# Spatial gating on Trainium2: the u projection and the token mixing with channels on the partitions

## The chip, the cores and the metric

The kernel runs on one core of one Trainium2 chip. The metric is the device time of one execution in microseconds (us). Engines: PE (TensorE; PEld are its weight loads), DVE (VectorE), ACT (ScalarE), POOL (GpSimd), SP (SyncE, which issues the DMAs). A matmul holds one operand of up to 128 x 128 still in the array, loaded ahead of it, and moves the columns of the other past it; the result goes to PSUM, here in banks of 128 x 512 f32.

## The reference

A trunk of two layers on 256 tokens of 1024 channels. Each layer is SwiGLU, a mixer, SwiGLU, with a layer norm behind each. The mixer of the first layer is the spatial gating at issue:

```
z = gelu(x @ w_in + b_in)            # 256 x 4096
u, v = split(z, 2, axis=-1)          # 256 x 2048 each
v = layer_norm(v, ln_g, ln_b)
v = v.reshape(1, 2, 128, 16, 128)    # 2 chunks of 128 tokens, 16 groups of 128 channels
w = where(causal, w_sp, 0)           # 16 x 128 x 128, token by token
mixed = einsum('gts,bcsgd->bctgd', w, v) + b_sp.T[None, None, :, :, None]
out = (u * mixed.reshape(1, 256, 2048)) @ w_out
```

The mixer of the second layer is an RWKV-7 time mixing, which the change leaves alone.

## The kernel before, in words

**Products.** Weights are f32. A `Stream` brings them in units of 128 x 1024 in the order of their use: SP loads a unit (L90) into one of 4 staging tiles `raw`, ACT rounds it to fp32r (`wh`, L113) and DVE takes the rest (`wl`, L114). A ring of 4 places, with 6 more while there is room, holds the split units; a staging tile is free again, and the next load may start, when its unit is split. Activations are split likewise (`split`, L206 to L208). `mm3` (L199 to L203) makes a product of three fp32r matmuls: rounded by rounded, and twice rounded by rest.

**Order.** The stage is written as a list of ops; `run` issues them in order, and ahead of each splits the units that have a place. PE and SP execute in this order. The order on ACT and DVE is set by the scheduler, so a wait on either holds what is queued behind it.

**The spatial gating (`sgu`, L440 to L620).** Tokens are on the partitions, in two blocks `m` of 128. `to_cm` (L218) transposes x for use as the still operand: `xh`, `xl`, channels by tokens. `proj_both` (L304) makes 512 columns of a projection for both blocks in four quarters, each with two of the four units of a part: block 0, block 1, block 0, block 1. The still operand is x (128 channels by 128 tokens), and 512 weight columns move past it. There are two PSUM banks `mm` for this, so each part needs the banks of the part before.

1. Four parts of v (key `sv`): `vdone` (L482) adds the bias on DVE, applies GELU on ACT, and gathers statistics; `vln` normalises v in place, four times two passes over 1024 columns (L252, L253).
2. Four parts of u (key `su`, p = 0 to 3): `udone` (L513) adds the bias on DVE (L521) and applies GELU on ACT (L522).
3. `M(p)` (L525): per token block, four products of a group's transposed causal weights `wspT` with v, in f32 (L532; each shows as two matmuls in the trace), into a bank `tp`; then four fused steps on DVE, (mixed + b_sp) * u, with b_sp one number per token, that is per partition (L538).
4. `T(p)` (L542): the gated u is transposed for the output projection, 8 transposes (L547), and split on ACT and DVE (L207, L208) into `pT`.
5. `O(p, i, m)` (L553): six matmuls with `pT` as the still operand and 512 columns of w_out moving, accumulating into four banks `acc`.

M and T of a part stand between quarters of later parts, or between O's.

Of the kernel before, what the change touches and what calls it, by code (L numbers as in the profile page):

```python
# [22 lines left out]
P = 128  # L23
D = 1024
# [30 lines left out]
class Stream:  # L55
    """Weight units in the order of their use: each is loaded ahead of time and split
    exactly into a rounded part and the rest, which one-pass products carry."""
# [12 lines left out]
    def free(self, now, v):  # L70
        """The next place of the ring for unit v, if the work issued up to op `now` is done with it."""
        shut = min((i for i in self.shut if i > now), default=1 << 30)
        n = N_W + (N_WX if self.ext and self.last[v] < shut else 0)
        for d in range(n):
            t = (self.turn + d) % n
            u = self.ring[t]
            if u is None or self.last[u] <= now:
                return t
        return None

    def load(self, now, upto=None):
        """Load what the staging places allow after the work issued up to op `now`."""
        while len(self.loaded) < (upto or len(self.units)):
            v = len(self.loaded)
            o = v - N_RAW
            if o >= 0 and (len(self.done) <= o or o in self.native and self.last[o] > now):
                break
            t = self.raw.tile([P, 1024], F32, tag="raw", name=f"raw{v}")
            for view, src in self.units[v]:
                self.nc.sync.dma_start(view(t), src)  # L90
            self.loaded.append(t)

    def advance(self, now, ahead, upto=None):
# [24 lines left out]
        assert upto is None or upto < len(self.done), "no place for a weight unit"  # L118
# [4 lines left out]

class Builder:
# [14 lines left out]
    def extra(self, kind):  # L139
        """The room next to the lasting pools: more weight units, or more 4 KB tiles."""  # L140
# [11 lines left out]
    def flush(self):  # L152
        """The last normalisation of the stage before, behind the first work of this one."""
# [64 lines left out]
    def to_cm(self, src):  # L218
        """[tokens, channels] -> rounded part and rest, [channel, block of channels, token]."""
# [52 lines left out]
    def proj(self, ps, m, xs, key, us):  # L272
        """ps[128 tokens, 512] += x[m] @ units us of key (two blocks of 128 rows each)."""
        for u in us:
            h, l = self.w((key, u))
            for k in range(2):
# [5 lines left out]
                else:  # L282
                    i = self.mm3(ps, xs[0][:, c], xs[1][:, c], h[:, s], l[:, s], kk == 0, kk == 7)
# [20 lines left out]
    def proj_both(self, key, xs, done, between=None):  # L304
        """Both token blocks, two units at a time; between[i]: ops before the i-th quarter."""
# [134 lines left out]
    def sgu(self, S):  # L440
# [9 lines left out]
        st = {"xs": [None, None], "p": {}, "pT": {}, "u": {}, "n": [0, 0], "bc": {}}  # L450

        def cm(m):
            def f():
                st["xs"][m] = self.to_cm(S["x"][m])
# [7 lines left out]
        def start2():  # L462
# [6 lines left out]
            bs = self.small("bsp", [16, P])  # L469
            nc.sync.dma_start(bs, a["sgu_b_sp"][0])  # L470
            st["wsp"], st["bsn"] = wsp, bs
# [6 lines left out]
        def start4():  # L478
            st["bu"] = [self.bcast(bin_[h * D:(h + 1) * D], "bu") for h in range(2)]
# [27 lines left out]
        def bspT():  # L507
            ps = self.tpb()
            nc.tensor.transpose(ps[:, :16], st["bsn"], self.ident[:16, :16])
            st["bsp"] = self.small("bspT", [P, 16])  # L510
            nc.vector.tensor_copy(st["bsp"], ps[:, :16])

        def udone(p):  # L513
            def f(m, ps):
                if (p, 0) not in st["u"]:
                    t = self.s4("u")
                    for mm in range(2):
                        st["u"][p, mm] = t[:, mm * 512:mm * 512 + 512]
                u = st["u"][p, m]
                h, s = p // 2, slice((p % 2) * 512, (p % 2) * 512 + 512)  # L520
                nc.vector.tensor_tensor(u, ps, st["bu"][h][:, s], op=ALU.add)  # L521
                nc.scalar.activation(u, u, AF.Gelu)  # L522
            return f

        def M(p):  # L525
            def f():
                for m in range(2):
                    ps = self.tpb()
                    for i in range(4):
                        g = 4 * p + i  # L530
                        o = slice((g % 8) * P, (g % 8) * P + P)
                        nc.tensor.matmul(ps[:, i * P:i * P + P], lhsT=st["wT"][g // 8][:, o],  # L532
                                         rhs=st["v"][m][g // 8][:, o], start=True, stop=True)
                    for i in range(4):
                        g = 4 * p + i
                        s = slice(i * P, i * P + P)
                        u = st["u"][p, m][:, s]
                        nc.vector.scalar_tensor_tensor(u, ps[:, s], st["bsp"][:, g:g + 1], u,  # L538
                                                       op0=ALU.add, op1=ALU.mult)
            return f  # L540

        def T(p):  # L542
            def f():
                for m in range(2):
                    ps = self.tpb()
                    for i in range(4):
                        nc.tensor.transpose(ps[:, i * P:i * P + P], st["u"][p, m][:, i * P:i * P + P], self.ident)  # L547
                    t = self.s4("pT", F32R)
                    self.split(t[:, 0:512], t[:, 512:1024], ps)
                    st["pT"][p, m] = t  # L550
            return f

        def O(p, i, m):  # L553
            def f():
                t = st["pT"][p, m]
                n0 = st["n"][m]
                wh, wl = self.w(("so", 4 * p + i))
                for n in range(2):
                    s = slice(n * 512, n * 512 + 512)
                    self.mm3(st["acc"][m][n], t[:, i * P:i * P + P], t[:, 512 + i * P:512 + i * P + P],  # L560
# [25 lines left out]
        self.proj_both(("sv", 3), xs, vdone(3), {1: [bspT]})  # L586
# [5 lines left out]
        def group(p, m_, t_):  # L592
            for i in range(4):
                O(p, i, 0)
                O(p, i, 1)
                if i == 0:
                    self.op(m_)
                if i == 2:
                    self.op(t_)
# [23 lines left out]
    def rwkv(self, S):  # L623
        """The loads and the preparation that may come before the stage, and the stage."""
# [106 lines left out]
        def lora1(m):  # L731
            """The first products of both small nets, with a row of ones below for the second's bias."""
# [35 lines left out]
        def decay_x(m):  # L768
            """What stood before each token: the row above, or 1 at the start of a chunk."""
# [8 lines left out]
        def decay_w(m):  # L778
            """A chunk's last row is the decay of the whole chunk."""
# [131 lines left out]
        def cm_kb(m, i, q):  # L911
            """Chunk 0 has its keys before its b's, chunk 1 behind."""
# [146 lines left out]
        class Chunk:  # L1059
            """One chunk of 64 tokens; v's in the half of the partitions that is the chunk's, u's in the other."""  # L1060
# [308 lines left out]
```

## Time and profile before

| what | value |
|---|---|
| median of 3 runs | 1148.21 us (1146.11 to 1149.02) |
| profiled execution, span from first to last instruction | 1146.8 us |
| PE busy | 1103.2 us, 96% |
| weight loads busy (PEld) | 878.3 us, 77% |
| DVE busy | 698.1 us, 61% |
| ACT busy | 481.2 us, 42% |
| DMA, mean | 189 GB/s |
| granted TensorE clock, mean over the span | 0.987 |

The profile is one execution of its own. Its span is 1146.8 us, and the time of that execution from outside is not among the numbers shown; the runs' median lies 1.4 us above the span, their lowest 0.7 below it. A busy time is the union of an engine's records. Records of matmuls, and of weight loads, overlap: the mean of one says how long it was under way, and the distance between starts says what it cost. The granted clock is 1.00 at 2.4 GHz and 0.50 at 1.2 GHz.

### The profile page before, as it was taken

The numbers are of one execution on the slowest core, as the hardware profiler recorded it, in microseconds if no ns is written. First come the engines' busy times: TensorE is split into PE (matmuls) and PEld (weight loads), VectorE is DVE, ScalarE is ACT, GpSimd is POOL, SyncE is SP. The second block draws the span as 40 slices with busy tenths as digits, with TensorE's granted clock in tenths as the row PEclk, the third lists the DMA queues.
The fourth block names the chain that finished last, engine by engine and source line by source line (L and its number), as shares of the span: only waits on it lengthen the run. The fifth ranks groups of instructions, "written<-read, shape, count | busy, mean of one in ns | idle before, by whom it ended". The sixth has DMA issues, their size and how long they took to land.

```text
span 1146.8 us, 15330 instructions
## 1 busy us (share of the span) xinstructions
PE 1103.2 (96%) x5854; PEld 878.3 (77%) x5854; DVE 698.1 (61%) x964; ACT 481.2 (42%) x632; POOL 42.3 (4%) x44
## 2 busy tenths in 40 slices
PE   7999999999999999999999999999989889999997
PEld 5788888778888888888788888775555768888885
DVE  5654556769658555457655453878655788555544
ACT  5544444455335444444444452462123145444430
POOL 0000000100000000000000000112100110000000
PEclk9999999999999999999999999999998999999999
DMA  8776565776644766655567563437876135766631
GB/s 277 244 236 187 182 196 168 233 254 201 215 147 151 243 204 199 187 184 154 189 218 224 184 199 125 165 93 251 269 203 222 60 123 190 245 201 196 184 111 37
DMA packets 153788, 216.51 MB, mean 189 GB/s; under 512 B 21197, under 2 KB 114829, under 8 KB 153714
## 3 DMA queue, kind: packets, MB, share of 16 engines
q1 hardware_dynamic: 152250, 210.80, 57.5%
q0 software_dynamic: 1024, 3.15, 1.0%
q10 hardware_dynamic: 440, 1.57, 0.5%
q8 instruction: 46, 0.75, 0.3%
q14 instruction: 28, 0.23, 0.1%
HBM read 209.46 MB, written 3.42 MB: 186 GB/s over the span
## 4 chain that ended last, share of the span: by engine, by line
PE 77%; DVE 8%; DMA 7%; issue 3%; ACT 2%; SPq 1%; POOL 1%; ACTq 0%; DVEq 0%; POOLq 0%
PE mm L201 14%; PE mm L203 14%; PE mm L202 14%; PE acc L201 8%; PE acc L203 8%; PE acc L202 8%; PE mm L281 3%; DMA raw<-ffn_w_in 3%; DVE wl L114 2%; PE tp L376 2%; ACT wh L113 1%; DMA raw<-sgu_w_in 1%; POOL rs L239 1%; SPq L90 1%; PE tp L215 1%
## 5 line engine op out<-in xcount | busy, mean ns | idle before, releaser
L114 DVE TENSOR_TENSOR wl<-raw,wh 128x1024 fp32r<-128x1024 f32 x328 | 396.2, 1221 | 272.7 <-ACT wh L113 264.7
L113 ACT CAST wh<-raw 128x1024 fp32r<-128x1024 f32 x328 | 340.4, 1051 | 347.7 <-PE acc L203 144.1
L201 PE MATMUL mm<-wh,xh 128*128 128x512 f32 x832 | 327.6, 394 | 8.3 <-DVE h L366 3.8
L202 PE MATMUL mm<-wl,xh 128*128 128x512 f32 x832 | 325.1, 391 | 1.2 <-DVE wl L114 1.2
L203 PE MATMUL mm<-wh,xl 128*128 128x512 f32 x832 | 325.1, 391 | 0.2 <-DVE xl L208 0.2
L201 PEld LDWEIGHTS mm<-wh,xh 128*128 128x128 f32 x832 | 156.6, 188 | 44.9 <-DVE h L366 5.5
L202 PEld LDWEIGHTS mm<-wl,xh 128*128 128x128 f32 x832 | 156.6, 188 | 34.8 <-DVE wl L114 3.2
L203 PEld LDWEIGHTS mm<-wh,xl 128*128 128x128 f32 x832 | 156.5, 188 | 34.4 <-DVE xl L208 1.9
L201 PE MATMUL acc<-wh,hT 128*128 128x512 f32 x352 | 140.9, 400 | 0.0
L203 PE MATMUL acc<-wh,hT 128*128 128x512 f32 x352 | 137.6, 391 | 0.0
L202 PE MATMUL acc<-wl,hT 128*128 128x512 f32 x352 | 137.2, 390 | 0.0
L365 ACT ACTIVATE h<-mm 128x256 f32<-128x256 f32 x88 | 33.8, 384 | 104.1 <-PE mm L203 104.1
L203 PEld LDWEIGHTS acc<-wh,hT 128*128 128x128 f32 x352 | 66.1, 188 | 14.3
L202 PEld LDWEIGHTS acc<-wl,hT 128*128 128x128 f32 x352 | 66.3, 188 | 12.8
L201 PEld LDWEIGHTS acc<-wh,hT 128*128 128x128 f32 x352 | 66.1, 188 | 12.5
L366 DVE TENSOR_TENSOR h<-h,mm 128x256 f32<-128x256 f32 x88 | 36.7, 417 | 58.8 <-ACT h L365 58.8
L281 PE MATMUL mm<-raw,mix 128*128 128x512 f32 x128 | 60.6, 619 | 0.7 <-DMA raw<-rwkv_w_rkv 0.7
L239 POOL TENSOR_TENSOR rs<-ve,mhalf 128x1 f32<-128x1 f32 x14 | 14.1, 1010 | 928.0 <-DVE ve L247 928.0
L281 PEld LDWEIGHTS mm<-raw,mix 128*128 128x128 f32 x128 | 24.0, 196 | 27.2 <-issue 25.1
L208 DVE TENSOR_TENSOR hT<-tp,hT 128x512 fp32r<-128x512 f32 x44 | 30.1, 684 | 7.6 <-ACT hT L207 7.6
L207 ACT CAST hT<-tp 128x512 fp32r<-128x512 f32 x44 | 25.8, 587 | 9.0 <-PE tp L376 8.9
L261 DVE SCALAR_TENSOR_TENSOR y<-acc,x 128x512 f32<-128x512 f32 x24 | 15.9, 685 | 18.7 <-PE acc L203 18.7
(189 smaller groups left out, 878.4 us busy)
## 6 DMA issues: line engine op xcount, KB each, us to landing
raw<-ffn_w_in SPq DMA_DIRECT2D x352, 256.0 KB, 3.9
raw<-ffn_w_out SPq DMA_DIRECT2D x88, 512.0 KB, 3.9
raw<-rwkv_w_rkv SPq DMA_DIRECT2D x40, 512.0 KB, 4.0
raw<-sgu_w_in SPq DMA_DIRECT2D x32, 512.0 KB, 4.9
raw<-sgu_w_out SPq DMA_DIRECT2D x16, 512.0 KB, 3.5
raw<-rwkv_w_o SPq DMA_DIRECT2D x8, 512.0 KB, 3.5
lng<-ln_g SPq DMA_DIRECT2D x6, 512.0 KB
lnb<-ln_b SPq DMA_DIRECT2D x6, 512.0 KB
```

What stands on the lines that cost most here:

```text
L113: nc.scalar.copy(h, raw)
L114: nc.vector.tensor_tensor(l, raw, h.bitcast(F32), op=ALU.subtract)
L201: i = mm(out, lhsT=lh, rhs=rh, start=start, stop=False)
L202: mm(out, lhsT=lh, rhs=rl, start=False, stop=False)
L203: mm(out, lhsT=ll, rhs=rh, start=False, stop=stop)
L207: self.nc.scalar.copy(h, src)
L208: self.nc.vector.tensor_tensor(l, src, h.bitcast(F32), op=ALU.subtract)
L239: self.nc.gpsimd.tensor_tensor(rs, v, self.mhalf[:, :w], op=ALU.pow)
L281: i = self.nc.tensor.matmul(ps, lhsT=xs[:, c], rhs=h[:, s], start=kk == 0, stop=kk == 7)
L365: nc.scalar.activation(hb[:, o + 256:o + 512], ps[:, 0:256], AF.Silu)
L366: nc.vector.tensor_tensor(hb[:, o:o + 256], hb[:, o + 256:o + 512], ps[:, 256:512], op=ALU.mult)
L376: nc.tensor.transpose(ps[:, o:o + P], st["h"][c][:, hh:hh + P], self.ident)
```

## The change

The u projection changes sides. The weights are the still operand (128 channels of input by 128 columns of u, one group), and the 256 tokens of both blocks move past them, so u comes out with channels on the partitions. For this x is kept as a `Pair`: four tiles that hold both token blocks beside each other; the v projections read one block of them as before. `U(p)` takes the place of `proj_both` and `udone`: two ops of 48 matmuls, one for units 0 and 1, one for 2 and 3, each over the four groups of the part; two groups share a bank. In the second op GELU follows each group on ACT, from PSUM, with b_in as its bias per partition. `M(p, j)` mixes two groups of both token blocks with v as the still operand, so that the result has channels on the partitions too; DVE adds b_sp (now broadcast over the partitions, as b_in was), multiplies by u, and the product is split straight into `pT`. `T` is gone. The loads of b_in and b_sp change places.

```diff
+class Pair:
+    def __init__(self, b):
+        self.b = b
+        self.h = [b.s4("xh", F32R) for q in range(2)]
+        self.l = [b.s4("xl", F32R) for q in range(2)]
+
+    def fill(self, src, m):
+        def evac(q, ps):
+            at = lambda t: t.rearrange("p (k m t) -> p k m t", k=4, m=2)[:, :, m, :]
+            self.b.split(at(self.h[q]), at(self.l[q]), ps.rearrange("p (k t) -> p k t", k=4))
+        self.b.transpose8(src, evac)
...
+    def both(self, k):
+        o = (k % 4) * 256
+        return self.h[k // 4][:, o:o + 256], self.l[k // 4][:, o:o + 256]
...
-            st["bu"] = [self.bcast(bin_[h * D:(h + 1) * D], "bu") for h in range(2)]
+            bsp = a["sgu_b_sp"][0].rearrange("g t -> (g t)")
+            st["bsp"] = [self.bcast(bsp[h * D:(h + 1) * D], "bsb") for h in range(2)]
...
+        def U(p, between=None):
+            ps = []
+            def go(us):
+                def f():
+                    if us[0] == 0:
+                        ps[:] = [self.mmb(), self.mmb()]
+                        st["u"][p] = self.s4("u")
+                    ws = [self.w((("su", p), u)) for u in us]
+                    for g in range(4):
+                        out = ps[g // 2][:, (g % 2) * 256:(g % 2) * 256 + 256]
+                        for u, (h, l) in zip(us, ws):
+                            for k in range(2):
+                                xh, xl = st["X"].both(2 * u + k)
+                                c = slice(k * 512 + g * P, k * 512 + g * P + P)
...
+                                mm(out, lhsT=h[:, c], rhs=xh, start=first, stop=False, skip_group_check=True)
+                                mm(out, lhsT=l[:, c], rhs=xh, start=False, stop=False, skip_group_check=True)
+                                mm(out, lhsT=h[:, c], rhs=xl, start=False, stop=last, skip_group_check=True)
+                        if us[-1] == 3:
+                            o = g * 256
+                            nc.scalar.activation(st["u"][p][:, o:o + 256], out, AF.Gelu,
+                                                 bias=st["bu"][:, 4 * p + g:4 * p + g + 1])
+                return f
...
-        def T(p):
...
-                        nc.tensor.transpose(ps[:, i * P:i * P + P], st["u"][p, m][:, i * P:i * P + P], self.ident)
...
+        def M(p, j):
+            def f():
+                ps = self.tpb()
+                for i in range(2):
+                    g = 4 * p + 2 * j + i
+                    c = slice((g % 8) * P, (g % 8) * P + P)
+                    for m in range(2):
+                        o = (i * 2 + m) * P
+                        nc.tensor.matmul(ps[:, o:o + P], lhsT=st["v"][m][g // 8][:, c],
+                                         rhs=st["wT"][g // 8][:, c], start=True, stop=True)
...
+                nc.vector.tensor_tensor(e4(x), e4(ps), b.unsqueeze(2).broadcast_to([P, 2, 2, P]), op=ALU.add)
+                u = st["u"][p][:, j * 512:j * 512 + 512]
+                nc.vector.tensor_tensor(u, u, x, op=ALU.mult)
+                t = self.s4("pT", F32R)
+                self.split(t[:, 0:512], t[:, 512:1024], u)
+                st["pT"][p, j] = t
...
-        self.proj_both(("su", 0), xs, udone(0), {1: [vln(0, 0)], 2: [vln(0, 1)], 3: [vln(1, 0)]})
-        self.proj_both(("su", 1), xs, udone(1), {1: [vln(1, 1)]})
-        self.proj_both(("su", 2), xs, udone(2), {1: [M(0)], 3: [T(0)]})
+        U(0, {1: [vln(0, 0), vln(0, 1)]})
+        U(1, {0: [vln(1, 0)], 1: [vln(1, 1)]})
+        U(2, {0: [M(0, 0)], 1: [M(0, 1)]})
...
-        group(0, M(1), T(1))
-        self.proj_both(("su", 3), xs, udone(3), {1: [M(2)], 3: [T(2)]})
+        group(0, M(1, 0), M(1, 1))
+        U(3, {0: [M(2, 0)], 1: [M(2, 1)]})
         self.op(gb)
         self.ahead = 99
-        group(1, M(3), T(3))
+        group(1, M(3, 0), M(3, 1))
```

**PE, from the end of the second u part into the third.** Before, the mixing block of part 0 (L532; `vz` is v, `wspT` the causal weights) stands after the first quarter of the third part, and a block of transposes (L547) after its third:

```order
L203 MATMUL mm<-wh_2129,xl_1604 128x512
L532 MATMUL tp<-vz_1593,wspT_1696 128x128 [waits PE_49]
L532 MATMUL tp<-vz_1593,wspT_1696 128x128 x3
L532 MATMUL tp<-vz_1595,wspT_1696 128x128 x4
L201 MATMUL mm<-wh_2123,xh_1723 128x512 [waits DVE_49]
...
L203 MATMUL mm<-wh_2169,xl_1604 128x512
L547 MATMUL tp<-ident,u_2098 128x128 [waits DVE_49,Activation_49]
L547 MATMUL tp<-ident,u_2098 128x128 x3
```

Now half a block (L589) stands ahead of the third part, whose matmuls are 256 columns wide (L565 to L567):

```order
L567 MATMUL mm<-xl_1606,wh_2014 128x256
L589 MATMUL tp<-wspT_1698,vz_1593 128x128 [waits DVE_49,PE_49]
L589 MATMUL tp<-wspT_1698,vz_1595 128x128 [waits DVE_49]
L589 MATMUL tp<-wspT_1698,vz_1593 128x128
L589 MATMUL tp<-wspT_1698,vz_1595 128x128
L565 MATMUL mm<-xh_1603,wh_2171 128x256
L566 MATMUL mm<-xh_1603,wl_2172 128x256
L567 MATMUL mm<-xl_1605,wh_2171 128x256
```

The block moved ahead of the part's first matmul and was halved, and the transposes have no successor.

**ACT, from the second u part on.** Before (L113 rounds a weight, L522 is GELU of u, L207 the split of the transposed product; numbers tell tiles apart):

```order
L113 CAST wh_2260<-raw_2167 128x1024 [waits DMAHW7_49,PE_49,Activation_49]
L113 CAST wh_2266<-raw_2173 128x1024 [waits DMAHW0_49,PE_49,Activation_49]
L522 ACTIVATE u_2187<-u_2187 128x512 [waits DVE_49]
L113 CAST wh_2317<-raw_2208 128x1024 [waits DMAHW1_49,PE_49,Activation_49]
L113 CAST wh_2353<-raw_2214 128x1024 [waits DMAHW2_49,PE_49,Activation_49]
```

Now (L570 is GELU, from the bank `mm` and with the bias):

```order
L113 CAST wh_2317<-raw_2181 128x1024 [waits DMAHW6_49,Activation_49]
L570 ACTIVATE u_2185<-mm,bspT 128x256 [waits PE_49,Pool_49]
L113 CAST wh_2385<-raw_2240 128x1024 [waits DMAHW7_49,Activation_49]
L570 ACTIVATE u_2185<-mm,bspT 128x256 [waits PE_49]
L113 CAST wh_2391<-raw_2246 128x1024 [waits DMAHW0_49,Activation_49]
L570 ACTIVATE u_2185<-mm,bspT 128x256 [waits PE_49]
L113 CAST wh_2449<-raw_2315 128x1024 [waits DMAHW1_49,PE_49,Activation_49]
```

GELU was two passes that waited for DVE and freed no bank; it is now four that wait for PE and free PE's banks, each behind the copy of a weight that waits for a DMA.

## Rows read from the trace of the kernel before

**Rows 1.** Page's head: span, and each engine's busy us (share) xinstructions

```profile
span 1146.8 us, 15330 instructions
...
PE 1103.2 (96%) x5854; PEld 878.3 (77%) x5854; DVE 698.1 (61%) x964; ACT 481.2 (42%) x632; POOL 42.3 (4%) x44
```

**Rows 2.** Stretch: length; PE, PEld, DVE, ACT, POOL busy; clock, DMA, GB/s

```profile
251.00:327.00 76.00, 75.95 (x383) 63.81 (x382) 61.43 (x90) 36.17 (x44) 2.91 (x2) 1.00 0.60 198
```

**Rows 3.** Chain of waits from 190 to 360 us: start us, us, what

```profile
276.55 1.78 PE tp L532 x16
...
283.80 0.87 PE tp L547 x8
...
324.56 0.87 PE tp L547 x8
```

**Rows 4.** Timeline of PE, first two u parts: start us, us, engine, line

```profile
253.85 0.39 PE L203 MATMUL mm<-wh,xl 128*128 128x512 f32 x1
254.18 0.50 PE L201 MATMUL mm<-wh,xh 128*128 128x512 f32 x1
254.52 0.39 PE L202 MATMUL mm<-wl,xh 128*128 128x512 f32 x1
...
262.25 0.39 PE L203 MATMUL mm<-wh,xl 128*128 128x512 f32 x1
262.69 0.47 PE L201 MATMUL mm<-wh,xh 128*128 128x512 f32 x1
263.00 0.40 PE L202 MATMUL mm<-wl,xh 128*128 128x512 f32 x1
```

**Rows 5.** Timeline of PE at a mixing block and at a transpose block

```profile
276.39 1.95 PE L532 MATMUL tp<-vz,wspT 128*128 128x128 f32 x16
278.09 0.48 PE L201 MATMUL mm<-wh,xh 128*128 128x512 f32 x1
278.41 0.40 PE L202 MATMUL mm<-wl,xh 128*128 128x512 f32 x1
...
283.64 1.03 PE L547 MATMUL tp<-ident,u 128*128 128x128 f32 x8
...
284.74 0.40 PE L202 MATMUL mm<-wl,xh 128*128 128x512 f32 x1
```

**Rows 6.** Weight loads by line: xcount | busy us, mean ns | idle before, releaser

```profile
L202 PEld LDWEIGHTS mm<-wl,xh 128*128 128x128 f32 x832 | 156.6, 188 | 34.8 <-DVE wl L114 3.2
...
L532 PEld LDWEIGHTS tp<-vz,wspT 128*128 128x128 f32 x64 | 7.8, 191 | 0.3
```

**Rows 7.** DVE and ACT groups, the same view

```profile
L113 ACT CAST wh<-raw 128x1024 fp32r<-128x1024 f32 x328 | 340.4, 1051 | 347.7 <-PE acc L203 144.1 <-PE mm L203 126.3 <-DMA raw<-ffn_w_in 30.0
...
L365 ACT ACTIVATE h<-mm 128x256 f32<-128x256 f32 x88 | 33.8, 384 | 104.1 <-PE mm L203 104.1
...
L538 DVE SCALAR_TENSOR_TENSOR u<-tp,bspT,u 128x128 f32<-128x128 f32 x32 | 8.8, 343 | 4.7 <-PE tp L532 4.7
...
L521 DVE TENSOR_TENSOR u<-mm,bu 128x512 f32<-128x512 f32 x8 | 5.5, 685 | 1.2 <-PE mm L203 1.2
...
L522 ACT ACTIVATE u<-u 128x512 f32<-128x512 f32 x8 | 5.0, 632 | 4.9 <-DVE u L521 4.8
```

**Rows 8.** Timelines of DVE and ACT, 253 to 270 us

```profile
253.44 0.68 DVE L486 TENSOR_TENSOR vz<-mm,bv 128x512 f32<-128x512 f32 x1
...
259.47 2.47 DVE L253 SCALAR_TENSOR_TENSOR vz<-vz,rs,slb 128x1024 f32<-128x1024 f32 x2
...
261.86 0.68 DVE L521 TENSOR_TENSOR u<-mm,bu 128x512 f32<-128x512 f32 x1
...
268.06 1.22 DVE L114 TENSOR_TENSOR wl<-raw,wh 128x1024 fp32r<-128x1024 f32 x1
...
269.44 1.05 ACT L113 CAST wh<-raw 128x1024 fp32r<-128x1024 f32 x1 [5.40 <-DMA raw<-sgu_w_out]
```

**Rows 9.** DMA issues, 200 to 327 us: xcount, KB each, median us to landing

```profile
raw<-sgu_w_out SPq DMA_DIRECT2D x16, 512.0 KB, 3.5
```

More of the change, by code (lines that the diff above doesn't have):

```diff
@@ L121, in get, with block, at @@
         return self.done[i]
+class Pair:
[8 more added lines that the diff above has]
+        self.b.transpose8(src, evac)
+    def block(self, m):
+        def at(k):
+            o = (k % 4) * 256 + m * P
+            return self.h[k // 4][:, o:o + P], self.l[k // 4][:, o:o + P]
+        return at
+    def both(self, k):
+        o = (k % 4) * 256
+        return self.h[k // 4][:, o:o + 256], self.l[k // 4][:, o:o + 256]
 class Builder:
@@ L282, in proj @@
                 else:
-                    i = self.mm3(ps, xs[0][:, c], xs[1][:, c], h[:, s], l[:, s], kk == 0, kk == 7)
+                    xh, xl = xs(kk) if callable(xs) else (xs[0][:, c], xs[1][:, c])
+                    i = self.mm3(ps, xh, xl, h[:, s], l[:, s], kk == 0, kk == 7)
                 self.first.setdefault(key, i)
@@ L449, in sgu @@
             self.def_rows(("so", g), wout[g * P:(g + 1) * P, :])
-        st = {"xs": [None, None], "p": {}, "pT": {}, "u": {}, "n": [0, 0], "bc": {}}
+        st = {"xs": [None, None], "pT": {}, "u": {}, "n": [0, 0]}
         def cm(m):
             def f():
-                st["xs"][m] = self.to_cm(S["x"][m])
+                if m == 0:
+                    st["X"] = Pair(self)
+                st["X"].fill(S["x"][m], m)
+                st["xs"][m] = st["X"].block(m)
             return f
@@ L468, in start2 @@
                                         base=0, channel_multiplier=1)
-            bs = self.small("bsp", [16, P])
-            nc.sync.dma_start(bs, a["sgu_b_sp"][0])
-            st["wsp"], st["bsn"] = wsp, bs
+            bu = self.small("bsp", [16, P])
+            nc.sync.dma_start(bu, bin_[0:DSGU].rearrange("(g p) -> g p", p=P))
+            st["wsp"], st["bun"] = wsp, bu
             st["wT"] = [self.s4("wspT") for h in range(2)]
@@ L505, in wspT, with buT @@
             return f
-        def bspT():
+        def buT():
             ps = self.tpb()
[L509 to L523, printed above, removed]
@@ L525, in M @@
-        def M(p):
-            def f():
[L527 to L540, printed above, removed]
@@ L542, in T @@
-        def T(p):
[L543 to L546, printed above, removed]
-                        nc.tensor.transpose(ps[:, i * P:i * P + P], st["u"][p, m][:, i * P:i * P + P], self.ident)
-                    t = self.s4("pT", F32R)
-                    self.split(t[:, 0:512], t[:, 512:1024], ps)
-                    st["pT"][p, m] = t
+            nc.tensor.transpose(ps[:, :16], st["bun"], self.ident[:16, :16])
+            st["bu"] = self.small("bspT", [P, 16])
@@ new lines, in buT @@
+            nc.vector.tensor_copy(st["bu"], ps[:, :16])
+        def U(p, between=None):
[12 more added lines that the diff above has]
+                                c = slice(k * 512 + g * P, k * 512 + g * P + P)
+                                mm = self.nc.tensor.matmul
+                                first = u + k == 0 and g % 2 == 0
+                                last = u == 3 and k == 1 and g % 2 == 1
+                                mm(out, lhsT=h[:, c], rhs=xh, start=first, stop=False, skip_group_check=True)
[7 more added lines that the diff above has]
+            for i in range(2):
+                for fn in (between or {}).get(i, ()):
+                    self.op(fn)
+                us = [2 * i, 2 * i + 1]
+                self.op(go(us), *[(("su", p), u) for u in us])
@@ new lines, in M @@
+        def M(p, j):
+            def f():
+                ps = self.tpb()
+                for i in range(2):
+                    g = 4 * p + 2 * j + i
[4 more added lines that the diff above has]
+                                         rhs=st["wT"][g // 8][:, c], start=True, stop=True)
+                g = 4 * p + 2 * j
+                e4 = lambda t: t.rearrange("p (g m t) -> p g m t", g=2, m=2)
+                b = st["bsp"][g // 8][:, (g % 8) * P:(g % 8) * P + 2 * P].rearrange("p (g t) -> p g t", g=2)
+                x = self.small("X", [P, 512])
+                nc.vector.tensor_tensor(e4(x), e4(ps), b.unsqueeze(2).broadcast_to([P, 2, 2, P]), op=ALU.add)
[4 more added lines that the diff above has]
+                st["pT"][p, j] = t
```

15 lines of the change are left out of this document (7 added, 8 removed).

## The prediction

> **What bounds the kernel now.** I read the head of the page first: one core, a span of 1146.8 us, PE busy for 96% of it, every other compute engine below two thirds; PEld, the weight loads beside PE, has 77% [rows 1]. Busy shares hide where the limit lies, so I cut the stage in stretches: between 251 and 327 us, where the u projection, the mixing and the first three quarters of the output projection run, PE is busy for 75.95 of 76.00 us at a granted clock of 1.00 (the 2.4 GHz level), while DVE has 61.43 and ACT 36.17 [rows 2]. The chain of waits agrees: the long pieces of it between 254 and 325 us are PE's matmuls, among them the mixing and the transposes, and none is a DMA's, DVE's or ACT's [rows 3]. So in this stretch a microsecond saved on PE's own list is a microsecond of time, and work taken from DVE or ACT is worth nothing by itself. A matmul's record is longer than its turn (records overlap), so costs on PE are taken from starts: 34 turns lie between the starts at 254.52 and 262.25 us, 0.227 us each [rows 4].
>
> The profiled execution's span is 1146.8 us; the median of the three runs is 1148.2, 1.4 above it, the lowest 1146.1. The difference worked out below is put on the median.
>
> **The change part by part.**
>
> *Transposes removed.* One block of 8 transposes starts at 283.64 and the second matmul behind it at 284.74: 1.10 us, less one turn of 0.227, is 0.87 us [rows 5]. There are four blocks: **-3.5 us**, all of it on PE's path.
>
> *The u projection.* Before: 4 parts x 8 row blocks x 2 token blocks x 3 products = 192 matmuls of 512 columns, 192 x 0.227 = 43.6 us. After: 4 x 8 x 4 groups x 3 = 384 of 256 columns, each with a weight load of 128 columns of its own. No row shows an fp32r matmul of 256 columns. At 2.4 GHz 512 columns take 0.2133 us, so a turn has 0.0137 us on top [rows 4]. If that belongs to the instruction, a turn of 256 columns is 0.1067 + 0.0137 = 0.1204 us and the projection 46.2 us: +2.6. If it belongs to the columns, a turn is 0.1135 and the cost 0. The lowest turn for a pair of a 128-column load and 256 clocks of streaming is that of the mixing matmuls, 128 columns of f32 at two clocks each: from 276.39 to 278.41, less the one turn of 0.227, 1.79 / 16 = 0.112 us [rows 5], which would give 43.0 us, -0.6. The upper end is a load that can't overlap the one before: its record is 188 ns [rows 6], so 384 x 0.188 = 72.2 us, +28.6. I take 0.1204, **+2.6 us**, because twice as many instructions is what the change makes and the row nearest in type is the fp32r one; both ends stay for the range and the rivals.
>
> *Mixing.* The same 32 f32 products, in eight blocks of 4 where there were four of 8. A block of before costs 2.02 - 0.227 = 1.79 us [rows 5]; half as much twice is the same. The first fp32r turn behind a block is 0.32 where 0.227 is usual [rows 5]; if that were lost four more times it would be +0.4. I take **0**.
>
> *Waits of PE in the u projection.* Turns at 253.85 and 254.18 are 0.33 and 0.34, at 262.25 and 262.69 0.44 and 0.31: 0.51 us over four usual ones [rows 4]. The first is the second mm bank, which DVE's bias add of the last v part gives back late, at 253.44 + 0.68, behind weight splits [rows 8]. The first u matmul stands near 253.85 - 11 x 0.227 = 251.35, and the new loop asks for the second bank after 24 turns, at 254.24 in place of 254.08, so it no longer waits. The second is the first bank of the next part, which DVE's bias add at 261.86 gave back late, right behind four passes over v (the last two are the 2.47 us at 259.47) [rows 8]. That add is gone; GELU reads the bank on ACT, with the bias in it, half a part before PE asks again. **-0.5 us.**
>
> *DVE and ACT.* DVE loses 8 bias adds (685 ns) and 32 fused steps (343 ns, 8.8 us together), and gains 16 passes of 512 (685 ns each as the nearest row): about -3 us. ACT has 16 GELUs of 256 columns (384 ns as the ffn's, also from PSUM) for 8 of 512 (632 ns): +1.1 us; its split of the product is moved, not added [rows 7]. I cost both at nothing: PE's 75.95 us cover them [rows 2]. Were PE not the longer, ACT's +1.1 would be the price. The strided writes of x's split stand at the stage's start, where PE does wait for them; no row has that form, the nearest are plain passes of 512, 632 ns on ACT and 685 on DVE [rows 7], so 0, and at most one more pair of those, +1.3.
>
> *Loads.* The two 512 KB broadcasts of b_in become two of b_sp, and the 8 KB load changes its source; SP issues as many, at the same places among the weights. The four tiles for x's split are taken at once rather than two and two; in the printed order no engine gets a new wait from it. 0.
>
> *Order.* The new mixing block has its data early: its v passes end on DVE near 268 us, and it is due near 274. The output projection asks for a product's split two or more of its own steps later (1.36 us for six turns each), against four DVE and ACT passes of 0.6 to 0.7 us. What is late next is therefore PE's own list again.
>
> **Sum:** -3.5 + 2.6 + 0 - 0.5 = -1.4 us, 0.12% of the time; from 1148.2 to **1146.8**. About 0.3% (3.4 us) is what a measurement of this kernel can tell from no change. The cut of 32 transposes is nearly bought back by 192 more instructions.
>
> **Rivals.**
>
> 1. *The extra 14 ns don't come along* (faster). With a turn of 0.112 to 0.1135 the sum is -4.6 to -4.0. For it: the f32 mixing pairs do run at 0.112 with loads of 191 ns [rows 5, 6]. Against: every fp32r turn here has the 14 ns. PE then reaches the third u part at 251.35 + 21.5 + 0.9 = 273.8, near 0.5 us before its bank is free (below), so -4.1 to -3.5, about 1144.4. The Trainium skill ("TensorE: Matmul & The Clock Gate", section "Back-to-back issue gap") gives N/2.4 + 2.5 ns: 109 ns for 256 columns, by which the projection would take 41.9 us and the sum be -5.7. By the same rule 512 columns take 216 ns where the rows have 227, so here the measurement decides.
>
> 2. *The weight load becomes the bound* (slower). In the old projection each load hides beside a matmul of twice its columns; in the new one a load of 128 columns stands against 256 clocks. If fp32r loads can't follow each other faster than their 188 ns record, the sum is +28.6 - 4.0 = +24.6, 1172.8. It decides from a turn of (43.6 + 4.0) / 384 = 0.124 us, and is measurable from 0.133. Against: the f32 loads of 191 ns follow at 0.112 [rows 5, 6]. For: no fp32r load has yet been asked to. The same page, section "LDWEIGHTS", has columns/1.2 GHz, 107 ns for 128 columns, just under my 0.1204; by that rule this rival falls away, and the 0.112 of the f32 pairs agrees.
>
> 3. *GELU behind a weight copy* (a wait in the place of one removed). On ACT each GELU of the second u part now stands behind a copy of a weight that must first land. The split that frees the first such load ended at 268.06 + 1.22 before [rows 8]; in the new order two adds are gone ahead of it and one more pass over v (2.47 / 2) stands there instead, so about 269.3 again; with a load of 3.5 us, a copy of 1.05 and GELU's 0.38 the bank is free at 274.3, and PE asks at 251.35 + 2 x 11.56 + 0.90 = 275.4 [rows 7, 8, 9]. Slack 1.1 us. ACT did wait 5.40 us there for a load before [rows 8]; if that comes on top, PE waits 4.3, and the time is 1151.1.
>
> 4. *It doesn't do what it says:* if 256 columns don't run in one fp32r pass but at f32's two passes of two clocks, a turn is four times 0.1067 = 0.43 us, +120: 1266. Nothing in the trace points to it; none of its fp32r matmuls is this narrow.
>
> **Numbers.** Forecast 0.56, rival 1 0.24, rival 2 0.08, rival 3 0.09, rival 4 0.03. Faster by over 0.3%: most of rival 1 and the forecast's lower edge, 0.23. Slower: rivals 2 and 4 and half of 3, with the strided writes' bound, 0.16. The rest, 0.61, is no change that can be told. The range takes in rival 1 with its lower bound (1143.3) and rival 3 (1151.1); it leaves out rivals 2 and 4 and a few in 100 below, together under 0.2.
>
> **What would show it.** Right: 384 matmuls in the u projection with starts 0.120 apart; no transposes of u; PE without gaps from the first u part to the output projection; that stretch, 76 us before, about 1.4 shorter. Turns of 0.113 with no gap make rival 1 true; turns above 0.124 rival 2; a gap on PE before the third part that ends with ACT's GELU rival 3. A difference that arises in another stage would mean that I have not seen what the change does.

## The result: 1.1% slower, all of it in the u projection

| | before | changed |
|---|---|---|
| median | 1147.16 us (1144.63 to 1149.02, 4 runs) | 1160.45 us (1159.93 to 1160.73, 4 runs) |
| ratio | | 1.0114 (95%: 1.0096 to 1.0132) |
| span of the profiled execution | 1146.8 us | 1158.7 us (its time 1160.46) |
| first u matmul to next SwiGLU ("the stretch") | 251.35 to 349.80: 98.45 us | 249.40 to 361.62: 112.22 us |

The forecast was 1146.8 us, no change that can be told. The stretch, which takes in the u projection, the mixing and the output projection, is 13.8 us longer; the 797 us behind it are equal within 0.2 us, and the v part ahead of it is 1.6 shorter. In a second pair of traces (e5 and e6, below) the stretch differs by 12.9 us, the part behind it by 3.5 the other way (795.7 before, 792.2 changed): the loss in the stretch comes back, the equality behind it does not.

The head of the page of the changed kernel answers to [rows 1]: PE has the same share, and 160 matmuls more (192 from the narrower u products, less 32 transposes).

```profile
span 1158.7 us, 15620 instructions
...
PE 1107.3 (96%) x6014; PEld 888.5 (77%) x6014; DVE 695.7 (60%) x940; ACT 484.3 (42%) x640; POOL 42.2 (4%) x44
```

The share hides the loss, as the stretches show. The changed kernel, cut at the u parts' ends and then the whole stretch (columns as in [rows 2]):

```profile
249.40:284.00 34.60, 31.71 (x258) 30.89 (x257) 28.34 (x31) 17.96 (x24) 2.91 (x2) 1.00 0.67 213
284.00:292.00 8.00, 5.23 (x32) 5.03 (x32) 3.83 (x5) 1.97 (x4) 0.00 (x0) 0.79 0.41 133
292.00:316.00 24.00, 23.44 (x154) 21.32 (x154) 14.09 (x17) 10.69 (x13) 0.00 (x0) 1.00 0.52 176
316.00:328.00 12.00, 8.67 (x47) 8.04 (x46) 3.10 (x5) 2.60 (x6) 0.00 (x0) 0.72 0.28 87
249.40:361.60 112.20, 102.64 (x641) 93.32 (x640) 71.32 (x82) 46.49 (x59) 3.83 (x3) 0.95 0.51 161
```

Before, PE was busy for 98.40 of these 98.45 us:

```profile
251.35:349.80 98.45, 98.40 (x482) 82.33 (x481) 74.76 (x107) 43.24 (x50) 3.83 (x3) 1.00 0.56 183
```

Now it is idle for 9.6 of 112.20, and in two pieces of it the granted clock is below 1.00. The waits of PE from 249 to 330 us are one line (us in total, times, longest):

```profile
PE mm L565 <- ACT u L570: 9.6, 8, 2.8
```

All eight are waits of the u projection for ACT's GELU of u. The groups of the stretch (as [rows 6, 7]):

```profile
L565 PE MATMUL mm<-xh,wh 128*128 128x256 f32 x128 | 39.3, 307 | 9.6 <-ACT u L570 9.6
...
L570 ACT ACTIVATE u<-mm,bspT 128x256 f32<-128x256 f32 x16 | 7.6, 472 | 18.0 <-PE mm L567 18.0
...
L595 DVE TENSOR_TENSOR X<-tp,bsb 128x512 f32<-128x512 f32 x8 | 5.5, 688 | 3.4 <-PE tp L589 3.4
L597 DVE TENSOR_TENSOR u<-u,X 128x512 f32<-128x512 f32 x8 | 5.5, 685 | 0.0
```

ACT is idle for 18.0 us waiting for PE in front of these GELUs, and PE for 9.6 waiting for ACT: the two engines work in turn. The timeline of PE in the second op of the first part shows where (columns as in [rows 4], with the idle time before and its releaser in brackets):

```profile
255.32 0.28 PE L566 MATMUL mm<-xh,wl 128*128 128x256 f32 x1
...
256.52 0.28 PE L567 MATMUL mm<-xl,wh 128*128 128x256 f32 x1
257.94 0.38 PE L565 MATMUL mm<-xh,wh 128*128 128x256 f32 x1 [1.14 <-ACT u L570]
258.17 0.28 PE L566 MATMUL mm<-xh,wl 128*128 128x256 f32 x1
...
260.80 0.28 PE L567 MATMUL mm<-xl,wh 128*128 128x256 f32 x1
261.64 0.39 PE L565 MATMUL mm<-xh,wh 128*128 128x256 f32 x1 [0.56 <-ACT u L570]
```

From 255.32 to 256.52 are 10 turns, 0.120 each. 256.52 ends group 0; the next matmul opens group 1, in the other half of the same bank, and it starts only when GELU has read group 0. 257.94 to 260.80 are the 24 matmuls of groups 1 and 2, in two banks, with no wait between them; 261.64 opens group 3, and waits for GELU of group 2. The wait stands in PE's printed order (row number first): 12 matmuls of group 0 lie ahead of this row, and 24 rows separate it from the next such one.

```
1085 L567 MATMUL mm<-xl_1606,wh_1960 128x256
1086 L565 MATMUL mm<-xh_1604,wh_1954 128x256 [waits Activation_49]
...
1110 L565 MATMUL mm<-xh_1604,wh_1954 128x256 [waits Activation_49]
```

Four parts have two such waits each. With ACT free, a wait is a turn of 0.84 us in place of 0.12. The one at 257.94 is 1.42: there GELU stands on ACT behind the copy of a weight that had waited for its load.

```profile
256.47 1.04 ACT L113 CAST wh<-raw 128x1024 fp32r<-128x1024 f32 x1 [0.23 <-DMA raw<-sgu_w_in]
257.42 0.47 ACT L570 ACTIVATE u<-mm,bspT 128x256 f32<-128x256 f32 x1
```

Twice it is 3.05: in the third and the fourth part, where the second mixing block (L589) has just been issued ahead of the op. PE, ACT and DVE in the third part:

```profile
285.23 0.28 PE L567 MATMUL mm<-xl,wh 128*128 128x256 f32 x1
288.28 0.58 PE L565 MATMUL mm<-xh,wh 128*128 128x256 f32 x1 [2.77 <-ACT u L570]
288.66 0.41 PE L566 MATMUL mm<-xh,wl 128*128 128x256 f32 x1
...
291.22 0.41 PE L566 MATMUL mm<-xh,wl 128*128 128x256 f32 x1
291.43 0.31 PE L567 MATMUL mm<-xl,wh 128*128 128x256 f32 x1
291.58 0.28 PE L565 MATMUL mm<-xh,wh 128*128 128x256 f32 x1
```

```profile
287.23 0.62 ACT L235 CAST pT<-u 128x512 fp32r<-128x512 f32 x1 [2.73 <-DVE u L597]
287.76 0.47 ACT L570 ACTIVATE u<-mm,bspT 128x256 f32<-128x256 f32 x1
```

```profile
284.73 0.68 DVE L595 TENSOR_TENSOR X<-tp,bsb 128x512 f32<-128x512 f32 x1
285.33 1.22 DVE L114 TENSOR_TENSOR wl<-raw,wh 128x1024 fp32r<-128x1024 f32 x1
286.46 0.68 DVE L597 TENSOR_TENSOR u<-u,X 128x512 f32<-128x512 f32 x1
```

Read it backwards. GELU could have read the bank just behind 285.23, and ACT was idle; but its next instruction was the split of the mixing product, which waited 2.73 us for DVE's multiplication, and that stood behind a weight split, behind the bias add. Everything in that chain is work that the forecast had costed at nothing.

After this wait the turns are 0.213 us, until 291.43; then 0.12 again. The granted clock is 0.5 (1.2 GHz) there, and once more from 318.8 us. Both falls, at 288.1 and 318.8 us, lie inside the two long waits, in each of which PE stood still for 2.77 us.

The sum against the kernel e1 below, whose stretch of 96.87 us has none of these waits: eight waits, from start to start and each less one usual turn, 11.0 us (9.6 of it shows as idle time, since records overlap); turns at the lower clock, 3.8 us (1.5 and 2.3); a slower first turn (0.22) behind the six other waits, 0.6 us. That is 15.4; the two stretches differ by 15.35.

### The profile page after: what moved, and what is told of

Read it like the earlier page. It is cut to its first block, busy times and chain, and to the rows that moved or that the text cites. A ratio compares the mean times of both kernels' runs of the same rounds, so it can differ in the third digit from the quotient of the medians.

```text
span 1158.7 us, 15620 instructions
## 1 busy us (share of the span) xinstructions
PE 1107.3 (96%) x6014; PEld 888.5 (77%) x6014; DVE 695.7 (60%) x940; ACT 484.3 (42%) x640; POOL 42.2 (4%) x44
## 4 chain that ended last, share of the span: by engine, by line
PE 78%; DVE 7%; DMA 6%; ACT 3%; issue 3%; POOL 1%; ACTq 0%; SPq 0%; DVEq 0%; POOLq 0%
PE mm L229 13%; PE mm L231 13%; PE mm L230 13%; PE acc L229 8%; PE acc L231 8%; PE acc L230 8%; PE mm L309 3%; DVE wl L114 2%; DMA raw<-ffn_w_in 2%; PE tp L405 2%; ACT wh L113 1%; DMA raw<-sgu_w_in 1%; PE mm L565 1%; DMA raw<-rwkv_w_rkv 1%; PE mm L566 1%
## 5 line engine op out<-in xcount | busy, mean ns | idle before, releaser
L113 ACT CAST wh<-raw 128x1024 fp32r<-128x1024 f32 x328 | 340.1, 1051 | 327.6 <-PE acc L231 144.9
L229 PE MATMUL mm<-wh,xh 128*128 128x512 f32 x768 | 302.5, 394 | 6.0 <-DVE h L395 2.7
L230 PE MATMUL mm<-wl,xh 128*128 128x512 f32 x768 | 300.6, 391 | 0.5 <-DVE wl L114 0.5
L231 PE MATMUL mm<-wh,xl 128*128 128x512 f32 x768 | 300.6, 391 | 0.2 <-DVE xl L236 0.2
L229 PEld LDWEIGHTS mm<-wh,xh 128*128 128x128 f32 x768 | 144.9, 189 | 38.6 <-DVE h L395 4.3
L230 PEld LDWEIGHTS mm<-wl,xh 128*128 128x128 f32 x768 | 144.8, 189 | 31.9 <-DVE wl L114 2.6
L231 PEld LDWEIGHTS mm<-wh,xl 128*128 128x128 f32 x768 | 144.8, 189 | 31.9 <-DVE xl L236 1.9
L565 PE MATMUL mm<-xh,wh 128*128 128x256 f32 x128 | 39.3, 307 | 9.6 <-ACT u L570 9.6
L566 PE MATMUL mm<-xh,wl 128*128 128x256 f32 x128 | 37.9, 296 | 0.0
L567 PE MATMUL mm<-xl,wh 128*128 128x256 f32 x128 | 37.8, 295 | 0.0
```

The lines of the kernel that those rows point to most:

```text
L229: i = mm(out, lhsT=lh, rhs=rh, start=start, stop=False)
L230: mm(out, lhsT=lh, rhs=rl, start=False, stop=False)
L231: mm(out, lhsT=ll, rhs=rh, start=False, stop=stop)
L565: mm(out, lhsT=h[:, c], rhs=xh, start=first, stop=False, skip_group_check=True)
L566: mm(out, lhsT=l[:, c], rhs=xh, start=False, stop=False, skip_group_check=True)
L567: mm(out, lhsT=h[:, c], rhs=xl, start=False, stop=last, skip_group_check=True)
```

## The experiments

In each, the stretch in the trace is given beside the time. **e1 to e4** ran with a kernel before of 1148.75 us (1143.64 to 1155.33, 35 runs), **e5 to e8** with 1147.75 (1145.44 to 1152.62, 20 runs), **e9 and e10** with 1147.27 (1144.24 to 1149.75, 13 runs).

**e1: GELU only when a bank is complete.** Both GELUs of a bank are issued behind the bank's second group.

```diff
-                        if us[-1] == 3:
-                            o = g * 256
-                            nc.scalar.activation(st["u"][p][:, o:o + 256], out, AF.Gelu,
-                                                 bias=st["bu"][:, 4 * p + g:4 * p + g + 1])
+                        if us[-1] == 3 and g % 2 == 1:
+                            for gg in (g - 1, g):
+                                o = gg * 256
+                                nc.scalar.activation(st["u"][p][:, o:o + 256],
+                                                     ps[gg // 2][:, (gg % 2) * 256:(gg % 2) * 256 + 256], AF.Gelu,
+                                                     bias=st["bu"][:, 4 * p + gg:4 * p + gg + 1])
```

> Both GELUs of a bank are issued behind the bank's second group, so PE no longer writes one half of a bank right after ACT was sent to read the other. Theory A (the added time is PE waiting, between the two groups of a bank, for GELU of the first, and the lower clock behind the two longest of these waits): the turns above the usual between groups, which add up to 15.5 us in the changed kernel's trace (waits of 1.40, 0.83, 0.89, 0.83, 3.19, 0.83, 3.19 and 0.96 us with their first turn, and 3.3 us of turns at the lower clock), go; 1160.5 - 15.5 = 1145.0, turns stay at 0.120, granted clock 1.00 through the stage. Theory B (narrow matmuls with a weight load each cost more than their starts show, or loads of weights come late): the time stays within 3 us of 1160.

1143.47 us (1141.05 to 1147.21, 12 runs), ratio 0.9951 (0.9931 to 0.997). The waits are gone, and with them the falls of the clock. The stretch:

```profile
249.06:345.93 96.87, 96.87 (x642) 89.23 (x640) 71.02 (x82) 45.76 (x59) 3.84 (x3) 1.00 0.58 187
```

The groups of the same lines, where L565 now has no idle time before it:

```profile
L565 PE MATMUL mm<-xh,wh 128*128 128x256 f32 x128 | 36.6, 286 | 0.0
...
L571 ACT ACTIVATE u<-mm,bspT 128x256 f32<-128x256 f32 x16 | 6.7, 468 | 5.3 <-PE mm L567 5.3
```

And ACT in the third part, at the place of the long wait: the order on it is as before, the first pair of GELUs still stands behind the split that waits for DVE, but PE has another bank to work on meanwhile.

```profile
283.21 0.62 ACT L235 CAST pT<-u 128x512 fp32r<-128x512 f32 x1 [1.95 <-DVE u L599]
283.74 0.83 ACT L571 ACTIVATE u<-mm,bspT 128x256 f32<-128x256 f32 x2
```

So the same 384 matmuls, the same GELUs and the same mixing, with two lines moved, are faster than both kernels. The loss is not in the new layout of the product but in when its banks are read.

**e2: neighbouring groups in different banks.** Groups 0 and 2 share a bank, 1 and 3 the other; GELU behind each group as in the changed kernel.

```diff
-                        out = ps[g // 2][:, (g % 2) * 256:(g % 2) * 256 + 256]
+                        out = ps[g % 2][:, (g // 2) * 256:(g // 2) * 256 + 256]
...
-                                first = u + k == 0 and g % 2 == 0
-                                last = u == 3 and k == 1 and g % 2 == 1
+                                first = u + k == 0 and g < 2
+                                last = u == 3 and k == 1 and g >= 2
```

> GELU stays behind each group, but groups 0 and 2 share a bank, and 1 and 3: between a GELU's group and the next write of its bank lies another group of 12 matmuls (1.44 us). Theory A, same-bank wait: the short waits of 0.83 us are covered, the two long ones of the third and fourth part (2.93 us from a group's end to the next start) shrink by 1.44 to about 1.5 each, the clock stays up; 1160.5 - 15.5 + 3.0 = 1148.0. Rival A2 (ACT simply can't give banks back fast enough, whatever the pairing): the waits stay in sum and only move one group on; above 1156.

1149.92 us (1147.54 to 1152.58, 10 runs), ratio 1.0006 (0.9985 to 1.0026); stretch 103.03. The short waits for the group just finished are gone, and the long ones have shrunk by the 12 turns that now lie between: 3.05 - 1.44 = 1.61, which is the distance measured twice. PE's waits of more than 1 us in it:

```profile
253.44 0.39 PE L565 MATMUL mm<-xh,wh 128*128 128x256 f32 x1 [1.24 <-DVE vz L519]
...
262.02 0.39 PE L565 MATMUL mm<-xh,wh 128*128 128x256 f32 x1 [1.13 <-ACT u L570]
...
288.59 0.39 PE L565 MATMUL mm<-xh,wh 128*128 128x256 f32 x1 [1.33 <-ACT u L570]
...
316.18 0.39 PE L565 MATMUL mm<-xh,wh 128*128 128x256 f32 x1 [1.33 <-ACT u L570]
```

PE's wait follows the bank and not the columns: the next group in the same bank waits, though its columns are others. (A bank is also one tile of the program here, so these runs can't tell a wait by bank from a wait by tile.) The edit has a price of its own, the first row: the second bank is asked for 12 turns earlier, before the bias add of the last v part gives it back. The second row is a GELU behind the copy of a weight (260.55 us on ACT) that had waited 1.19 us for its load. The time is 1.9 us above the 1148.0 expected and far from the rival's 1156. The granted clock stays at 1.00 in the stretch:

```profile
250.61:353.64 103.03, 98.00 (x641) 89.46 (x640) 71.12 (x82) 45.92 (x59) 3.83 (x3) 1.00 0.55 175
```

The Trainium skill ("PSUM — Partial Sum Buffer", section "PSUM bank collisions raise a hardware error") says that software must guard PSUM by bank (and quadrant of partitions), not by address, since another address of a bank that is being read collides too. The waits here go by that rule; that an unguarded access would collide no run here shows.

**e3: the second mixing block behind the op.** M(0, 1) and M(2, 1) are issued behind the second half of their part in place of ahead of it.

```diff
-        U(2, {0: [M(0, 0)], 1: [M(0, 1)]})
+        U(2, {0: [M(0, 0)]})
+        self.op(M(0, 1))
...
-        U(3, {0: [M(2, 0)], 1: [M(2, 1)]})
+        U(3, {0: [M(2, 0)]})
+        self.op(M(2, 1))
```

> The second mixing blocks of the first and third part are put behind the second half of the u part in place of ahead of it; nothing else is changed. Theory A's second half (the long waits come from ACT's queue, where GELU stands behind the split of the mixed product, which waits for DVE): the two waits of 3.19 us become 0.83 as the others, and the clock doesn't fall; 1160.5 - 2 x 2.36 - 3.3 = 1152.4, the eight short waits stay. Rival (the long waits come from late weights): no change of these waits, 1160.

1153.39 us (1147.02 to 1158.43, 10 runs), ratio 1.0038 (1.0015 to 1.0061); stretch 104.93, 7.3 shorter than the changed kernel's. The two long waits are now like the other six:

```profile
287.80 0.39 PE L565 MATMUL mm<-xh,wh 128*128 128x256 f32 x1 [0.56 <-ACT u L570]
...
315.53 0.39 PE L565 MATMUL mm<-xh,wh 128*128 128x256 f32 x1 [0.62 <-ACT u L570]
```

```profile
251.22:356.15 104.93, 98.92 (x642) 89.62 (x640) 71.32 (x82) 46.38 (x59) 3.83 (x3) 1.00 0.54 172
```

The clock stays at 1.00. The long waits and what the clock took behind them were thus 4.4 + 3.8 = 8.2 us of the stretch, less 0.8 by which one other wait, at 260.56 us, is longer here: a turn of 2.21, with GELU behind the copy of a weight that had waited 1.09 us for its load.

**e4 and e7: the price of a set of transposes.** In the kernel before, each of the 32 transposes is made twice (e4) or four times (e7).

```diff
-                        nc.tensor.transpose(ps[:, i * P:i * P + P], st["u"][p, m][:, i * P:i * P + P], self.ident)
+                        for _ in range(2):
+                            nc.tensor.transpose(ps[:, i * P:i * P + P], st["u"][p, m][:, i * P:i * P + P], self.ident)
```

> The kernel before, with each of the 32 transposes of the gated u made twice into the same place. If the removed transposes were worth their PE turns (0.109 us each), this is 32 x 0.109 = 3.5 us slower than before: 1147.2 + 3.5 = 1150.7. If they lay beside other work, no change.

1149.02 us (1147.09 to 1152.11, 10 runs), ratio 0.9998 (0.9978 to 1.0018): the 3.5 us that were expected don't show in the time. In the trace they do: the stretch lasts 101.96 us, 3.51 more, PE busy for 101.92 of it, and each block is 0.87 longer:

```profile
282.21 1.91 PE L548 MATMUL tp<-ident,u 128*128 128x128 f32 x16
283.87 0.48 PE L201 MATMUL mm<-wh,xh 128*128 128x512 f32 x1
284.18 0.40 PE L202 MATMUL mm<-wl,xh 128*128 128x512 f32 x1
```

From 282.21 to 284.18, less a turn of 0.227, are 1.74 us for 16 where it was 0.87 for 8 [rows 5].

> The kernel before, each of its 32 transposes of the gated u made four times, 96 more. If a microsecond on PE in this stretch is a microsecond of time and one set of transposes costs 3.5 us: the stretch lasts 98.4 + 10.5 = 108.9 us and the time is 10.5 above e5's, about 1158.5 to 1159.5. Rival (a later stage, waiting for its weights, gives part back, as the 3.5 us of the doubled transposes did not show in the time): the stretch is as long, the time rises by 7 or less.

1155.1 us (1152.86 to 1156.72, 5 runs), ratio 1.0057 (1.0037 to 1.0077), 6.8 us above e5's median: the rival's 7 or less, and not the 10.5 of the first account; the stretch lasts 108.92 us, 10.47 more than before's. The PE cost of 3.5 us a set holds in the stretch in both; by the time, both gain some 3 us elsewhere.

**e5, e6, e8: once more, side by side.** The kernel before, the changed kernel and e1, unchanged.

> The kernel before, unchanged, as a kernel of its own, for a second trace and a second set of times beside the reference runs. Theory (what e1 to e4 moved outside the stretch from the first u matmul to the next SwiGLU is variation from run to run): ratio 1.000 within 0.2%; the stretch lasts 98.4 us, as in the trace before, within 0.2; the v part ahead of it may differ from its 51.0 us by 1 to 3. Rival (the trace of before is typical, and its v part is slower in every execution for a reason of its own): v part 51.0 again.

1148.33 us (1144.86 to 1152.61, 10 runs), ratio 1.0004 (0.9988 to 1.002); stretch 98.44 us; v part 50.33 where it was 51.05.

> The changed kernel, unchanged, beside e5 and e8 on the same chip. Theory (PE's waits for GELU and the clock that falls in the two long ones are set by the order of the program, not by chance): the stretch from the first u matmul to the next SwiGLU lasts 112.2 us again, within 0.5, with the two waits of about 3 us in the third and fourth part at the same places; time 1160 to 1162. Rival (a wait of 3 us is an accident of one DMA's arrival): the stretch shortens by 3 or more.

1160.75 us (1157.07 to 1162.83, 4 runs), ratio 1.0108 (1.0079 to 1.0136); stretch 111.31 us, 0.9 shorter, with eight waits at the same instructions: 1.25, 0.84, 0.90, 0.88, 3.05, 0.84, 3.05 and 0.84 us from start to start. The two long ones are thus set by the program's order, not by one transfer's arrival. The first one is not: it was 1.42 and 1.25 in the two traces.

> The changed kernel with GELU issued after the second group of each bank, as in e1, beside e5 and e6 on the same chip. By the terms of the prediction the stretch from the first u matmul to the next SwiGLU is 98.4 - 3.5 + 2.6 - 0.5 = 97.0 us, e1 had 96.9; time 1.4 below e5's if nothing else differs. Rival (e1's 5.3 us below before were real): 4 to 6 below e5's.

1143.35 us (1139.28 to 1146.05, 10 runs), ratio 0.9957 (0.9939 to 0.9975); stretch 97.05 us, PE busy for all of it.

**e9 and e10: one instruction more.** e1, e2, e4, e7 and e8 all lie about 3 us below what their stretch says. To see whether any program but the two originals does, one transpose of the kernel before is made twice (e9), and one mixing product of the changed kernel (e10).

```diff
+                        for _ in range(2 if p == m == i == 0 else 1):
```

> The kernel before with one of its 32 transposes of the gated u made twice: a program that differs from before by one instruction of about 0.11 us in the stretch. Theory (the 3.4 us by which the variants e1, e2, e4, e7 and e8 lie under what their stretch says is not from the stretch, and any program other than before's own gets it): about 3 us faster than before, near 1144.5 to 1145.5. Rival (it belongs to what was changed in the stretch, by way of later stages): same time as before within 0.1%.

1148.21 us (1145.81 to 1152.45, 10 runs), ratio 1.0011 (0.9995 to 1.0028); stretch 98.57. The interval leaves out the 3 us that the theory wanted: it falls.

> The changed kernel with one of its 32 mixing products made twice, 0.22 us more at the most. Theory (as e9): about 3 us faster than the changed kernel's 1160.5 to 1160.8, near 1157.5, though its stretch is 112 us again. Rival: 1160.5 to 1161.0.

1158.74 us (1158.08 to 1161.27, 4 runs), ratio 1.0099 (1.0073 to 1.0126); stretch 111.69. Between the two expectations; it decides nothing.

All of them, against the kernel before of the same series (medians) and its stretch of 98.45 us:

| | stretch, us | against 98.45 | time against before | time less stretch |
|---|---|---|---|---|
| changed | 112.22 | +13.8 | +13.3 | -0.5 |
| e6, changed again | 111.31 | +12.9 | +13.0 | +0.1 |
| e10, changed + 1 | 111.69 | +13.2 | +11.5 | -1.8 |
| e5, before again | 98.44 | 0.0 | +0.6 | +0.6 |
| e9, before + 1 | 98.57 | +0.1 | +0.9 | +0.8 |
| e1 | 96.87 | -1.6 | -5.3 | -3.7 |
| e8, e1 again | 97.05 | -1.4 | -4.4 | -3.0 |
| e2 | 103.03 | +4.6 | +1.2 | -3.4 |
| e3 | 104.93 | +6.5 | +4.6 | -1.8 |
| e4 | 101.96 | +3.5 | +0.3 | -3.2 |
| e7 | 108.92 | +10.5 | +7.4 | -3.1 |

What the last column is stays open. In the traces the differences outside the stretch lie in the v part ahead of it (51.05 and 50.33 us in the two traces of before, 48.6 and 49.7 in those of e1 and e8) and in the mixer of the second layer, but each trace is one execution, and up to the stretch's first transposes the code of e4 and e9 is the same: their v parts are 48.8 and 50.8 us, so a difference of 2 us there comes without any difference of the program.

## Why the prediction was wrong, by its own steps

- **Transposes, -3.5 us: right.** e4 and e7 make the same 0.87 us a block, 3.5 a set, in the stretch.
- **The u projection, a turn of 0.1204 us, +2.6: right.** The starts are 0.120 apart, in the changed kernel and in e1. The 14 ns beyond the streaming belong to the instruction, and rivals 1 (0.1135), 2 (above 0.124) and 4 (0.43) are out. By the rule of 109 ns ("TensorE: Matmul & The Clock Gate" of the Trainium skill, section "Back-to-back issue gap", which itself calls it the gap of an isolated matmul) the 384 turns would take an estimated 4.2 us less than the 46.1 that 384 times 0.120 make. The 107 ns of the same page of the Trainium skill for a load of 128 columns (section "LDWEIGHTS") lie under the turn. The trace of e1 agrees: records of loads are 192 ns long and overlap, and no wait of PE for one is seen.
- **Mixing, 0: right.** e1's first block starts at 272.14 us, and the second matmul behind it at 273.15; less a turn, 0.89 us. Eight are 7.1 us, as four of 1.79 were.

```profile
272.14 1.06 PE L591 MATMUL tp<-wspT,vz 128*128 128x128 f32 x8
272.95 0.36 PE L565 MATMUL mm<-xh,wh 128*128 128x256 f32 x1
273.15 0.28 PE L566 MATMUL mm<-xh,wl 128*128 128x256 f32 x1
```

- **Waits of before, -0.5: right for the two that were named.** At the places of [rows 4] PE no longer waits, in the changed kernel and in e1, but for 0.06 us at the first. The sum of these four terms, -1.4, makes a stretch of 97.05 us: e1 has 96.87 and e8 97.05.
- **The step that failed** is the premise of that same part, "GELU reads the bank on ACT, with the bias in it, half a part before PE asks again", and with it "What is late next is therefore PE's own list again". It is true of the next part, which asks for the bank from its beginning. But PE asks for it in the same op too, one instruction later, for the bank's second group. That made eight turns of 0.84 us and more, 11.0 us over the usual ones, in the place of two waits that cost 0.5 together. The new order of PE shows them, row by row (above); the prediction read in it only what stands around the mixing block, and took the bank for one user's until the part ended.
- **"DVE and ACT ... I cost both at nothing: PE's 75.95 us cover them" failed with it.** Cover holds for work that nobody waits for. When PE waits for GELU, all that stands ahead of GELU on ACT is on the path, and what that waits for on DVE: the split, the multiplication, the weight split and the bias add made 3.05 us of 0.84, twice. e1 has nearly the same busy times on DVE and ACT (71.02 and 45.76 us in the stretch, where they were 71.32 and 46.49), and they are covered again.
- **Rival 3 named the right engine and the wrong place.** It put GELU behind a weight copy that waits for a load, and the gap before the third part; there is none there. PE met GELU in the middle of the part, and in the two long waits GELU was late behind a copy of another kind, which waited for DVE. What rival 3 described on ACT did happen once, in the first part (the turn of 1.42 us), and cost 0.6 us over a wait with ACT free. Its 4.3 us were one wait; there were eight, of 11.0 us. In e1, whose edit leaves the weight copies and the loads as they are, PE waits for neither.
- **The clock** was in no step: 3.8 us more.
- **The range** has a lower bound, 1143.3, that none of the prediction's sums gives: the lowest of them, -4.6, makes 1143.6. Nothing hangs on it, since the time lies far above the range.

## What to carry to other kernels

When two groups of an accumulation share a PSUM bank, read the bank when both are done: a read after the first makes PE wait for it, 0.72 us a time here with the reader idle, more when anything else stands in the reader's queue. "That engine is off the path" has to be asked again for every instruction of it that a changed loop makes PE wait for; PE's new order, gone through to the end of one whole turn of the loop, lists them. And a term of 1 to 4 us is read from a stretch of the trace, where it came out within 0.2 us here, while the time of the whole kernel moved by 3 us that are not in the stretch and whose cause stays open.

## What was not expected of the hardware

- GELU of 256 columns from PSUM takes 468 to 472 ns here, with a bias per partition; the prediction had taken 384 from the ffn's activation of the same shape [rows 7], which is another function (Silu) and has no bias. Which of the two makes the difference was not tried.
- With the two long waits of PE the granted clock fell to 0.5, and the turn of 256 columns went from 0.120 to 0.213 us, for 3.3 us in the third part and some 5 in the fourth. In e6's trace the falls come 0.9 and 0.3 us behind the end of the same waits. In e2 and e3, without those waits, it stayed at 1.00 in the stretch.
- 3.5 us of PE work added to the stretch (e4) did not lengthen the kernel measurably, and 1.5 taken out (e1) shortened it by 4 to 5. The cause wasn't found; e9 shows that not every difference of the program brings it.
